# High and low parts of a 128-column operand side by side in one matmul of 256 columns, in the attention heads of a two-block fp32 kernel

## The chip, the cores and the metric

One core of one Trainium2 chip runs the whole program. The metric is the device time of one execution in microseconds (us); lower is better. The chip's engines have an instruction stream each, run in program order, and wait for one another by semaphores: TensorE (PE in the rows: matmuls, PEld its weight loads), VectorE (DVE), ScalarE (ACT), GpSimd (POOL) and SyncE (SP), which here issues the transfers from memory.

## The reference

Two blocks on 256 tokens of width 1024, all in fp32. The first has differential attention (4 heads) beside block attention (8 heads, called moba), gates, and a gated per-layer input. The second has two layers of retention (4 heads, two blocks of 128 queries) beside stick-breaking attention (8 heads), and an MLP. Cut to what the change touches:

```python
def diff_attention(q, k, v, lam, ...):        # per head and query block
    a = softmax(where(causal, q @ k * scale, -inf))      # two maps, m = 0, 1
    w = a[:, :, 0] - lam * a[:, :, 1]
    o = rms_norm(w @ v, subln_g) * (1 - lam_init)

def retention(q, k, v, log_gamma):             # per head and 128-token chunk
    inner = ((q @ k) * decay) @ v
    cross = (q @ state) * q_decay

def stick_breaking(q, k, v):                   # per head
    z = q @ k * scale
    log_1m_beta = where(causal, log_sigmoid(z) - z, 0)
    after = reverse_cumsum(log_1m_beta) - log_1m_beta
    out = where(causal, exp(log_sigmoid(z) + after), 0) @ v
```

## The kernel before

**Numbers.** Every operand of a matmul is a sum of a high part (the value rounded to fp32r) and a low part (the rest). `hilo` makes them: ScalarE copies (line 131), VectorE subtracts (line 132). A product is then three matmuls, high x high, high x low, low x high, summed in PSUM; `mm3` (lines 139 to 142) issues them.

**Weights.** They come as 189 chunks of 1 MB into three buffers (`raw`), fetched by SyncE. Two chunks ahead of its use a chunk is split into `wh` (ScalarE, line 302) and `wl` (VectorE, line 303), with three buffers each. The chunk's matmuls (line 137) go into accumulators of one PSUM bank each (`acc`, five banks); a 512-column matmul multiplies a weight by high and low parts of the activations, which lie side by side, and one of 256 by the high part alone. The two halves of the bank are added afterwards: a ScalarE copy (line 337) and a VectorE addition (line 338), which make `f`.

**Heads.** The other three PSUM banks (`aux`) belong to the attention heads. Each head is a Python generator that is stepped once per chunk; its steps lie between `yield`s. `soft_head` (4 differential and 8 moba heads, one per 128 lanes), `ret_head` (8) and `sb_head` (16, 8 in each layer).

- A stick-breaking head: scores z by two `mm3`, 256 and 128 columns (two key blocks, causal); a mask added on both diagonal blocks; |z|, exp, ln on ScalarE; high and low part (`ph`, `pl`); then matmuls with a triangle and a vector of -1 (lines 796, 797: the reverse sum) into the same bank; an exponential; high and low part; values by two `mm3` (256 and 128 columns); and their high and low part into `B`, k = h for head h. `B` is what the chunk matmuls of p_sb multiply, all eight k's, so that heads 6 and 7 are waited for at k = 6 and 7.
- A differential head: values by `mm3` for each of three 128 x 128 blocks; squares with a sum (line 544, ScalarE reading PSUM), a power on GpSimd, scaling (line 548), and transposes (line 553).

**Order.** The program is handed to a scheduler that decides the order on each engine from a timeline that it computes itself. A change of a few instructions so moves many others. ScalarE's functions need tables; sigmoids need another one than exp and ln, and `act` emits the table load (line 116) ahead of the first one. The order of the functions with tables is kept as written.

Of the kernel before, what the change touches and what calls it, by code (L numbers as in the profile page):

```python
# [22 lines left out]
PB = 2  # L23
# [57 lines left out]
def tile_blocks(ctx: ExitStack, tc: tile.TileContext, a: dict, out: bass.AP):  # L81
# [61 lines left out]


# [13 lines left out]
    msk = tl([384], "msk")  # L158
    tri_f = tl([P], "sig", bufs=4)
# [9 lines left out]
    m_sb = msk[:, None, 2 * P:3 * P].to_broadcast([P, 2, P])  # L169
# [7 lines left out]
    def late_consts():  # L177
        load(cst, a["tables"][:, 0:C_SB])
        load(msk, a["tables"][:, C_SB:C_TRI])
        load(tri_f, a["tables"][:, C_TRI:C_DEC])  # L180
        load(lamv, a["lambdas"].rearrange("(o i e) -> o i e", o=1, e=64).to_broadcast([P, 4, 64]))

    def use_consts():
        V.tensor_mul(gfm, g_fin, g_mix[0])
        V.tensor_scalar_mul(subg, subg, 1.0 - LAM_INIT)
        V.tensor_copy(tri, tri_f)
        V.tensor_scalar_mul(neg1, ones, -1.0)
# [40 lines left out]
    def sums(sq, cols=True):  # L228
        h, l = tl([S], "ph", F32R, 2), tl([S], "pl", F32R, 2)
# [215 lines left out]
    def head_rows():  # L445

        for _ in range(3):
            yield
        ps = aux()[:, 0:S]
        for h in range(2):  # L450
            dh, dl = tl([P], "ph", F32R, PB), tl([P], "pl", F32R, PB)
# [40 lines left out]
    def soft_head(idx, j, v, diff, wait):  # L492
# [33 lines left out]
        wh, wl = tl([2, 384], "ph", F32R, 2), tl([2, 384], "pl", F32R, 2)  # L526
# [8 lines left out]
        if diff:  # L535
            po = aux()[:, 0:S].rearrange("p (h e) -> p h e", h=2)
            h, l = wh[:, 0], wl[:, 0]
            vc = slice(j * P, (j + 1) * P)
            for i, (o, qt, kt) in enumerate(BLK):
                mm3(po[:, qt], h[:, o:o + P], l[:, o:o + P], vh[:, kt, vc], vl[:, kt, vc], i == 0, qt == kt)  # L540
            o = o_slot[idx % 2]
            ss = tl([2], "ss", bufs=2)
            for h in range(2):
                A.activation(o[:, h], po[:, h], AF.Square, accum_out=ss[:, h:h + 1])
            V.tensor_scalar(ss, ss, 1.0 / 128, EPS5, ALU.mult, ALU.add)
            G.tensor_tensor(ss, ss, mhalf[:, 0:2], ALU.pow)
            for h in range(2):
                A.activation(o[:, h], po[:, h], AF.Copy, scale=ss[:, h:h + 1])
# [193 lines left out]
    def ret_head(h, j, qk, v, L):  # L742
        (qh, ql), (kh, kl) = qk
# [3 lines left out]
        mm3(ps[:, 256:384], kh[:, j, 128:256], kl[:, j, 128:256], qh[:, j, 128:256], ql[:, j, 128:256], False, True)  # L747
        t = tl([384], "t", bufs=2)
        V.tensor_mul(t, ps[:, 0:384], L.dec[:, 384 * h:384 * (h + 1)])
        dh, dl = tl([384], "ph", F32R, 2), tl([384], "pl", F32R, 2)  # L750
# [26 lines left out]
    def sb_head(h, j, qk, v, L):  # L777
        (qh, ql), (kh, kl) = qk
# [3 lines left out]
        mm3(z[:, 256:384], kh[:, j, 128:256], kl[:, j, 128:256], qh[:, j, 128:256], ql[:, j, 128:256], False, True)  # L782
        zd = z.rearrange("p (b s) -> p b s", b=2)[:, :, 0:P]
        V.tensor_add(zd, zd, m_sb)
# [6 lines left out]
        h2, l2 = tl([2, 384], "ph", F32R, 2), tl([2, 384], "pl", F32R, 2)  # L791
        h_, l_ = h2[:, 0], l2[:, 0]
# [7 lines left out]
        h_, l_ = h2[:, 1], l2[:, 1]  # L800
        hilo(h_, l_, t)
        yield
        po = aux()[:, 0:S]
        e = slice(h % 4 * P, (h % 4 + 1) * P)
        mm3(po, vh[:, 0, e], vl[:, 0, e], h_[:, 0:256], l_[:, 0:256], True, True)
        mm3(po[:, 128:256], vh[:, 1, e], vl[:, 1, e], h_[:, 256:384], l_[:, 256:384], False, True)
# [3 lines left out]
    def layer(l):  # L810
# [32 lines left out]
        for u in range(2):  # L843
# [3 lines left out]
            def ev(ps, h, u=u):  # L847
# [294 lines left out]
```

## Time and profile before

| | |
|---|---|
| time, median of three runs | 1152.4 us (1151.77 to 1152.56) |
| the profiled execution | 1152.48 us, its span 1150.5 us, mean granted clock 0.998 |
| TensorE busy | 1139.5 us (99%), 6579 matmuls |
| VectorE, ScalarE, GpSimd busy | 874.3 (76%), 717.7 (62%), 221.6 us (19%) |
| moved by DMA | 207.70 MB, mean 181 GB/s |

The span is the time between the first and the last instruction that the profile holds; some 2 us lie around it. The matmul's own time in the rows contains its way through the array, some 0.2 to 0.3 us, in which the next one already runs. What a matmul costs in a stream is the distance from its start to the next start.

### The profile page before, as it was taken

Reading aid. Unit: us, or ns where it says so; the run is one execution under the profiler, and the core shown is the slowest. Engines: PE = TensorE matmul, PEld = TensorE weight load, DVE = VectorE, ACT = ScalarE, POOL = GpSimd, SP = SyncE. Lnnn points to the kernel's source line nnn. Section 1 sums busy time; section 2 is a strip of 40 time slices with the busy share of each in tenths; the row PEclk is TensorE's granted clock in tenths of the full one; section 3 lists DMA queues with packets and bytes.
Section 4 is the critical chain, followed back from the end, with each engine's and each line's share of the span. In section 5 each row is a group of like instructions: output and inputs, shape, how many; then the busy total and the mean of one; then the engine's idle time right before and its main releaser. Section 6 shows DMA issues by size and latency. Waiting matters only on the chain.

```text
span 1150.5 us, 17428 instructions
## 1 busy us (share of the span) xinstructions
PE 1139.5 (99%) x6579; PEld 998.6 (87%) x6579; DVE 874.3 (76%) x1457; ACT 717.7 (62%) x1302; POOL 221.6 (19%) x236
## 2 busy tenths in 40 slices
PE   8999999999999999999999999999999999999997
PEld 6888899998888888888888888888898888888887
DVE  6867777689978867778876777978776767967664
ACT  7777955476567776556654645556776555856452
POOL 0021241036532122110000013641121312000001
PEclk9999999999999999999999999999999999999999
DMA  8644345556544445545555556455444654555551
GB/s 320 235 152 144 138 170 197 183 179 220 183 179 151 174 152 183 184 158 209 184 190 189 193 197 216 171 189 183 147 147 146 214 189 165 212 188 185 188 178 37
DMA packets 33028, 207.70 MB, mean 181 GB/s; under 512 B 3888, under 2 KB 6576, under 8 KB 8880
## 3 DMA queue, kind: packets, MB, share of 16 engines
q1 hardware_dynamic: 32944, 206.59, 50.9%
q8 instruction: 52, 0.85, 0.3%
q14 instruction: 32, 0.26, 0.1%
HBM read 203.42 MB, written 1.05 MB: 178 GB/s over the span
## 4 chain that ended last, share of the span: by engine, by line
PE 91%; DVE 4%; DMA 2%; ACT 2%; issue 1%; POOL 0%; SPq 0%; POOLq 0%; DVEq 0%
PE acc L137 80%; DVE wl L303 2%; PE acc L142 1%; PE acc L141 1%; PE acc L140 1%; PE aux L142 1%; PE aux L141 1%; PE aux L140 1%; DMA M<-in_xn_dram 1%; DVE X L688 1%; PE aux L797 1%; PE aux L501 1%; ACT wh L302 0%; POOL sig L838 0%; DMA X<-in_xt_dram 0%
## 5 line engine op out<-in xcount | busy, mean ns | idle before, releaser
L303 DVE TENSOR_TENSOR wl<-raw,wh 128x1024 fp32r<-128x1024 f32 (+1 forms) x382 | 466.3, 1248 | 114.4 <-ACT wh L302 111.8
L302 ACT ACTIVATE wh<-raw 128x1024 fp32r<-128x1024 f32 (+1 forms) x382 | 381.2, 1043 | 190.8 <-PE acc L137 159.2
L137 PE MATMUL acc<-X,wh 128*128 128x512 f32 x1472 | 382.9, 394 | 0.6 <-DVE X L688 0.4
L137 PEld LDWEIGHTS acc<-X,wh 128*128 128x128 f32 x1472 | 263.8, 189 | 49.0 <-issue 1.2
L137 PE MATMUL acc<-X,wl 128*128 128x256 f32 x1472 | 220.7, 283 | 0.0
L137 PEld LDWEIGHTS acc<-X,wl 128*128 128x128 f32 x1472 | 207.2, 190 | 14.1
L337 ACT ACTIVATE f<-acc 128x256 f32<-128x256 f32 x216 | 79.3, 374 | 69.1 <-PE acc L137 68.8
L137 PE MATMUL acc<-wh,X 128*128 128x512 f32 x448 | 118.8, 394 | 0.6 <-ACT wh L302 0.5
L338 DVE TENSOR_TENSOR f<-f,acc 128x256 f32<-128x256 f32 x216 | 87.3, 414 | 30.2 <-ACT f L337 29.3
L137 PEld LDWEIGHTS acc<-wh,X 128*128 128x128 f32 x448 | 83.3, 189 | 18.4 <-ACT wh L302 1.9
L220 POOL TENSOR_TENSOR sq<-sq,f 128x256 f32<-128x256 f32 x24 | 27.6, 1150 | 263.9 <-ACT f L218 263.7
L688 DVE TENSOR_TENSOR X<-X,acc 128x256 f32<-128x256 f32 x112 | 45.8, 416 | 34.2 <-PE acc L137 33.5
L619 POOL TENSOR_TENSOR sig<-f,nr 128x256 f32<-128x256 f32 x48 | 44.7, 940 | 120.1 <-DVE f L338 85.8
L137 PE MATMUL acc<-B,wh 128*128 128x512 f32 x256 | 64.7, 392 | 0.0
L137 PE MATMUL acc<-A,wh 128*128 128x512 f32 x256 | 64.4, 392 | 0.0
L137 PE MATMUL acc<-wl,X 128*128 128x512 f32 x224 | 64.4, 395 | 0.0
L137 PEld LDWEIGHTS acc<-B,wh 128*128 128x128 f32 x256 | 46.1, 189 | 8.2
L137 PE MATMUL acc<-M,wh 128*128 128x512 f32 x192 | 52.9, 393 | 0.0
L137 PEld LDWEIGHTS acc<-A,wh 128*128 128x128 f32 x256 | 45.9, 189 | 8.1
L137 PEld LDWEIGHTS acc<-wl,X 128*128 128x128 f32 x224 | 41.7, 188 | 9.1 <-DVE wl L303 1.0
L137 PEld LDWEIGHTS acc<-M,wh 128*128 128x128 f32 x192 | 35.0, 188 | 6.8
L568 POOL TENSOR_TENSOR G<-f,nr 128x256 f32<-128x256 f32 x24 | 22.7, 946 | 84.3 <-DVE f L338 83.9
(236 smaller groups left out, 1652.9 us busy)
## 6 DMA issues: line engine op xcount, KB each, us to landing
raw<-in_wstream_dram SPq DMA_DIRECT2D x187, 1024.0 KB, 4.8
sig<-f SPq DMA_DIRECT2D x32, 64.0 KB, 5.1
B<-in_tables_dram SPq DMA_DIRECT2D x2, 768.0 KB, 5.1
raw<-in_wstream_dram SPq DMA_DIRECT2D x4, 256.0 KB, 4.8
raw<-in_wstream_dram SPq DMA_DIRECT2D x2, 512.0 KB, 7.6
M<-in_xn_dram SPq DMA_DIRECT2D x1, 1024.0 KB, 11.4
out_dram<-M SPq DMA_DIRECT2D x4, 256.0 KB, 2.2
X<-in_xt_dram SPq DMA_DIRECT2D x3, 256.0 KB, 6.6
```

Source lines behind the costliest of these rows:

```text
L137: last[0] = T.matmul(*args, **kw)
L140: T.matmul(o, lhsT=lh, rhs=rh, start=start, stop=False, skip_group_check=True)
L141: T.matmul(o, lhsT=lh, rhs=rl, start=False, stop=False, skip_group_check=True)
L142: T.matmul(o, lhsT=ll, rhs=rh, start=False, stop=stop, skip_group_check=True)
L220: (V if k == KT - 1 else G).tensor_add(sq, sq, t)
L302: h = A.activation(ch.wh[:, k], ch.raw[:, k], AF.Copy)
L303: l = V.tensor_sub(ch.wl[:, k], ch.raw[:, k], f32(ch.wh[:, k]))
L337: A.activation(t, ps[:, S:2 * S], AF.Copy)
L338: V.tensor_add(t, t, ps[:, 0:S])
L568: G.tensor_mul(dst()[:, k], fold(ps), st.n.rb)
L619: G.tensor_mul(store[(c, i)][0][:, k % 2], fold(ps), st.n.rb)
L688: V.tensor_add(X[:, k], X[:, k], ps[:, o:o + S])
```

## The change

`mm2` takes the place of `mm3` where the moving operand has 128 columns. High and low part of that operand lie side by side ("ph" holds both now, the values too), and one matmul of 256 columns multiplies them by the stationary high part; its result is 256 columns wide, with the high product in one half and the low one in the other. A second matmul of 128 columns adds the product of the stationary low part. The two halves are summed behind it: `add_up` (ScalarE copies 128 columns, VectorE adds) in retention scores and stick-breaking values; in the stick-breaking scores a ScalarE copy into the tile "msb", a GpSimd addition of the mask to it, and the VectorE addition that was there before reads this tile; in the differential values a copy of 256 columns and an addition, after which the squares and the scaling read SBUF and not PSUM. The mask is loaded in a transfer of its own, 64 KB.

Score blocks of 8 retention and 16 stick-breaking heads, values of 16 stick-breaking heads, and values of 4 differential heads (three blocks each) are so changed. The moba heads are not.

```diff
+    def parts():
+
+        return tl([2, 2, 384], "ph", F32R, 2)
...
+    def mm2(o, o0, lh, ll, r, rh, start, stop):
+
+        T.matmul(o, lhsT=lh, rhs=r, start=start, stop=False, skip_group_check=True)
+        T.matmul(o0, lhsT=ll, rhs=rh, start=False, stop=stop, skip_group_check=True)
+
+    def add_up(o, ex, t):
+
+        A.activation(t, ex, AF.Copy)
+        V.tensor_add(o, o, t)
...
-    m_sb = msk[:, None, 2 * P:3 * P].to_broadcast([P, 2, P])
+    m_sb = tl([2, P], "msb")
...
-            po = aux()[:, 0:S].rearrange("p (h e) -> p h e", h=2)
+            po = aux().rearrange("p (h c e) -> p h c e", h=2, c=2)
...
-                mm3(po[:, qt], h[:, o:o + P], l[:, o:o + P], vh[:, kt, vc], vl[:, kt, vc], i == 0, qt == kt)
+                mm2(po[:, qt], po[:, qt, 0], h[:, o:o + P], l[:, o:o + P], v.v.t[:, kt, :, vc], vh[:, kt, vc],
+                    i == 0, qt == kt)
             o = o_slot[idx % 2]
             ss = tl([2], "ss", bufs=2)
+            A.activation(o, po[:, :, 1], AF.Copy)
+            V.tensor_add(o, o, po[:, :, 0])
+            q2 = tl([S], "ft", bufs=2)
             for h in range(2):
-                A.activation(o[:, h], po[:, h], AF.Square, accum_out=ss[:, h:h + 1])
+                A.activation(q2[:, h * P:(h + 1) * P], o[:, h], AF.Square, accum_out=ss[:, h:h + 1])
...
-                A.activation(o[:, h], po[:, h], AF.Copy, scale=ss[:, h:h + 1])
+                A.activation(o[:, h], o[:, h], AF.Copy, scale=ss[:, h:h + 1])
...
     def ret_head(h, j, qk, v, L):
...
-        mm3(ps[:, 256:384], kh[:, j, 128:256], kl[:, j, 128:256], qh[:, j, 128:256], ql[:, j, 128:256], False, True)
+        mm2(ps[:, 256:512].rearrange("p (c q) -> p c q", c=2), ps[:, 384:512], kh[:, j, 128:256], kl[:, j, 128:256],
+            qt_[:, j, :, 128:256], qh[:, j, 128:256], False, True)
         t = tl([384], "t", bufs=2)
+        add_up(ps[:, 256:384], ps[:, 384:512], t[:, 0:P])
...
     def sb_head(h, j, qk, v, L):
...
-        mm3(z[:, 256:384], kh[:, j, 128:256], kl[:, j, 128:256], qh[:, j, 128:256], ql[:, j, 128:256], False, True)
-        zd = z.rearrange("p (b s) -> p b s", b=2)[:, :, 0:P]
-        V.tensor_add(zd, zd, m_sb)
+        mm2(z[:, 256:512].rearrange("p (c q) -> p c q", c=2), z[:, 384:512], kh[:, j, 128:256], kl[:, j, 128:256],
+            qt_[:, j, :, 128:256], qh[:, j, 128:256], False, True)
+        zd, ms = z.rearrange("p (b s) -> p b s", b=2)[:, :, 0:P], m_sb
+        A.activation(ms[:, 1], z[:, 384:512], AF.Copy)
+        G.tensor_add(ms[:, 1], ms[:, 1], ms[:, 0])
+        V.tensor_add(zd, zd, ms)
...
-        mm3(po[:, 128:256], vh[:, 1, e], vl[:, 1, e], h_[:, 256:384], l_[:, 256:384], False, True)
+        mm2(p3[:, 128:384].rearrange("p (c q) -> p c q", c=2), p3[:, 256:384], vh[:, 1, e], vl[:, 1, e],
+            hl[:, 1, :, 256:384], h_[:, 256:384], False, True)
+        add_up(po[:, 128:256], p3[:, 256:384], tl([384], "t", bufs=2)[:, 0:P])
```

**Where instructions move.** Three places of the order on the engines follow. In the changed program line 140 is the chunk matmul, 143 to 145 are `mm3`, 149 and 150 `mm2`, 825 and 826 the triangular products, 134 and 135 `hilo`.

First, TensorE at the end of the stick-breaking heads of the first layer, before the change: aux_701 is the bank of head 7's values, acc_721 and acc_723 are the accumulators that multiply B, and acc_728, acc_731 and acc_736 belong to chunks that multiply X.

```order
L140 MATMUL aux_701_4530<-ph_680_4399,vh_638_4116 128x128
L141 MATMUL aux_701_4530<-pl_681_4400,vh_638_4116 128x128
L142 MATMUL aux_701_4530<-ph_680_4399,vl_639_4117 128x128
L137 MATMUL acc_728_4708<-X2_369_2428,wl_711_4591 128x256 x3
L137 MATMUL acc_731_4730<-X2_369_2428,wh_710_4590 128x512 x8
L137 MATMUL acc_731_4730<-X2_369_2428,wl_711_4591 128x256 x8
L137 MATMUL acc_721_4651<-B2_573_3683,wh_702_4539 128x512
L137 MATMUL acc_723_4676<-B2_573_3683,wh_702_4539 128x512
L137 MATMUL acc_736_4759<-X2_369_2428,wh_718_4643 128x512 x4
L137 MATMUL acc_721_4651<-B2_573_3683,wh_702_4539 128x512
L137 MATMUL acc_721_4651<-B2_573_3683,wl_703_4540 128x256 x8
L137 MATMUL acc_723_4676<-B2_573_3683,wh_702_4539 128x512
```

The same place in the changed program, from the last triangular product of head 7 on: aux_682 and aux_684 hold the values of heads 6 and 7, acc_705 and acc_707 multiply B, and the first row for B is k = 6, as is the second.

```order
L826 MATMUL aux_661_4384<-ph_663_4398,tri_10_73 128x384
L140 MATMUL acc_720_4761<-X2_363_2420,wl_703_4646 128x256 x5
L143 MATMUL aux_682_4519<-ph_660_4381,vh_623_4111 128x256
L144 MATMUL aux_682_4519<-ph_660_4381,vh_623_4111 128x256
L145 MATMUL aux_682_4519<-ph_660_4381,vh_623_4111 128x256
L149 MATMUL aux_682_4519<-ph_660_4381,vh_623_4111 128x256
L150 MATMUL aux_682_4519<-ph_660_4381,vh_623_4111 128x128
L143 MATMUL aux_684_4530<-ph_663_4398,vh_623_4111 128x256
L144 MATMUL aux_684_4530<-ph_663_4398,vh_623_4111 128x256
L145 MATMUL aux_684_4530<-ph_663_4398,vh_623_4111 128x256
L149 MATMUL aux_684_4530<-ph_663_4398,vh_623_4111 128x256
L150 MATMUL aux_684_4530<-ph_663_4398,vh_623_4111 128x128
```

The rows that come next are the two k = 6 matmuls of B and then the k = 7 one. The chunk matmuls on X that stood between the values and B (and between the triangular products and the values) now stand ahead of the triangular products.

Second, ScalarE at the same place in the changed program, from the exponential of head 6 (t_672) and of head 7 (t_673) on. The four sig tiles are gates; ph_663 is head 7's high part.

```order
L117 ACTIVATE t_672_4456<-aux_658_4367 128x384
L134 ACTIVATE ph_660_4381<-t_672_4456 128x384
L117 ACTIVATE t_673_4464<-aux_661_4384 128x384
L115 ACT_TABLE_LOAD
L117 ACTIVATE sig_650_4317<-sig_650_4317 128x512
L117 ACTIVATE sig_668_4426<-sig_668_4426 128x512
L117 ACTIVATE sig_678_4493<-sig_678_4493 128x512
L117 ACTIVATE sig_690_4566<-sig_690_4566 128x512
L134 ACTIVATE ph_663_4398<-t_673_4464 128x384
L154 ACTIVATE t_683_4525<-aux_682_4519 128x128
L134 ACTIVATE B2_559_3671<-aux_682_4519 128x256
L154 ACTIVATE t_685_4536<-aux_684_4530 128x128
```

Here is what stood there before, with head 6's and head 7's high parts ph_676 and ph_680.

```order
L118 ACTIVATE t_690_4458<-aux_674_4369 128x384
L118 ACTIVATE t_691_4466<-aux_678_4386 128x384
L116 ACT_TABLE_LOAD
L118 ACTIVATE sig_668_4323<-sig_668_4323 128x512
L131 ACTIVATE ph_676_4382<-t_690_4458 128x384
L118 ACTIVATE sig_686_4428<-sig_686_4428 128x512
L118 ACTIVATE sig_696_4495<-sig_696_4495 128x512
L337 ACTIVATE f_715_4618<-acc_713_4598 128x256
L118 ACTIVATE sig_706_4564<-sig_706_4564 128x512
L131 ACTIVATE ph_680_4399<-t_691_4466 128x384
```

Head 6's high part moved ahead of the table load; head 7's stands behind all four sigmoids in both orders, and the copies of line 154 are new.

Third, TensorE behind the values of the last differential head (aux_173 before), up to its transposes into aux_188.

```order
L142 MATMUL aux_173_977<-vh_79_440,pl_158_899 128x128
L137 MATMUL acc_179_1003<-wl_149_841,X2_13_76 128x512 x4
L137 MATMUL acc_179_1003<-wh_148_840,X2_13_76 128x512 x4
L137 MATMUL acc_178_1002<-wh_162_920,X2_13_76 128x512 x4
L137 MATMUL acc_178_1002<-wl_163_921,X2_13_76 128x512 x4
L137 MATMUL acc_178_1002<-wh_162_920,X2_13_76 128x512 x3
L553 MATMUL aux_180_1028<-cst_2_62,B2_15_78 128x128 x2
L137 MATMUL acc_178_1002<-wh_162_920,X2_13_76 128x512
L484 MATMUL aux_181_1034<-cst_2_62,sig_165_940 128x128 x4
L137 MATMUL acc_179_1003<-wh_162_920,X2_13_76 128x512 x4
L137 MATMUL acc_179_1003<-wl_163_921,X2_13_76 128x512 x4
L137 MATMUL acc_179_1003<-wh_162_920,X2_13_76 128x512 x4
```

Four more transposes of line 484 come next, and then those into aux_188. In the changed program the values are in aux_171 and the transposes go into aux_186 (line 576; line 502 is what line 484 was).

```order
L149 MATMUL aux_171_974<-vh_79_442,ph_156_896 128x256
L150 MATMUL aux_171_974<-vh_79_442,ph_156_896 128x128
L576 MATMUL aux_179_1025<-cst_2_62,B2_17_80 128x128 x2
L502 MATMUL aux_180_1031<-cst_2_62,sig_163_937 128x128 x4
L140 MATMUL acc_178_1000<-wl_161_918,X2_15_78 128x512 x2
L140 MATMUL acc_178_1000<-wh_160_917,X2_15_78 128x512 x4
L502 MATMUL aux_181_1038<-cst_2_62,sig_164_938 128x128 x4
L576 MATMUL aux_186_1082<-cst_2_62,B2_17_80 128x128
```

Between the values and these transposes 27 matmuls of 512 columns stood before, and 6 stand now. ScalarE's part of this chain in the changed program, from the new copy (line 563) over the squares (line 567) to the scaling (line 571), is this.

```order
L563 ACTIVATE B2_17_80<-aux_171_974 128x256
L431 ACTIVATE vh_185_1065<-acc_177_999,hr_30_148 128x512
L134 ACTIVATE M2_33_161<-aux_180_1031 128x2x256
L567 ACTIVATE ft_173_984,ss_172_981<-B2_17_80 128x128 x2
L134 ACTIVATE A2_19_82<-ft_152_878 128x256
L431 ACTIVATE vh_185_1065<-acc_178_1000,hr_30_148 128x512
L318 ACTIVATE wh_192_1118<-raw_162_923 128x1024 x2
L134 ACTIVATE M2_33_161<-aux_181_1038 128x2x256
L571 ACTIVATE B2_17_80<-B2_17_80,ss_172_981 128x128 x2
```

The copy is new, and two more evacuations of accumulators (line 431, 134) have come between the squares' input and the scaling than stood there before.

## Rows read from the trace of the kernel before

**Rows 1.** The page's first part: busy time, share of the span, instructions
```profile
PE 1139.5 (99%) x6579; PEld 998.6 (87%) x6579; DVE 874.3 (76%) x1457; ACT 717.7 (62%) x1302; POOL 221.6 (19%) x236
```
**Rows 2.** The chain that ended last, share of the span by engine
```profile
PE 91%; DVE 4%; DMA 2%; ACT 2%; issue 1%; POOL 0%; SPq 0%; POOLq 0%; DVEq 0%
```
**Rows 3.** Waits of TensorE, longest first: total us, times, longest
```profile
PE aux L428 <- DVE one_r L167: 1.3, 1, 1.3
...
PE aux L140 <- ACT M L131: 0.2, 1, 0.2
```
**Rows 4.** Timeline of TensorE, second layer's scores: start us, us, instruction
```profile
858.90 0.22 PE L140 MATMUL aux<-M 128*128 128x128 f32 x1
...
859.07 0.27 PE L142 MATMUL aux<-M 128*128 128x128 f32 x1
859.18 0.34 PE L141 MATMUL aux<-pl,vh 128*128 128x256 f32 x1
859.35 0.28 PE L142 MATMUL aux<-ph,vl 128*128 128x256 f32 x1
```
**Rows 5.** Timeline of TensorE, a moba head's values
```profile
135.22 0.28 PE L141 MATMUL aux<-pl,vh 128*128 128x256 f32 x1
135.34 0.28 PE L142 MATMUL aux<-ph,vl 128*128 128x256 f32 x1
```
**Rows 6.** Groups by line and shape, ScalarE: busy us, mean ns
```profile
L337 ACT ACTIVATE f<-acc 128x256 f32<-128x256 f32 x216 | 79.3, 374 | 69.1 <-PE acc L137 68.8
...
L544 ACT ACTIVATE B<-aux 128x128 f32<-128x128 f32 x8 | 2.1, 273 | 1.8 <-PE aux L142 1.8
```
**Rows 7.** Timeline of TensorE, first layer, end of the stick-breaking heads
```profile
425.63 0.39 PE L797 MATMUL aux<-pl,tri 128*128 128x384 f32 x1
...
440.08 0.39 PE L137 MATMUL acc<-B,wh 128*128 128x512 f32 x1
```
**Rows 8.** Timeline of ScalarE, the same stretch
```profile
425.66 0.89 ACT L118 ACTIVATE t<-aux 128x384 f32<-128x384 f32 x2 [1.85 <-PE aux L797]
426.57 1.28 ACT L116 ACT_TABLE_LOAD   x1
...
428.81 1.14 ACT L118 ACTIVATE sig<-sig 128x512 f32<-128x512 f32 x2
...
430.64 0.51 ACT L131 ACTIVATE ph<-t 128x384 fp32r<-128x384 f32 x1
...
435.69 0.38 ACT L131 ACTIVATE B<-aux 128x256 fp32r<-128x256 f32 x1 [0.90 <-PE aux L142]
```
**Rows 9.** Timeline of VectorE, the same stretch
```profile
431.19 0.79 DVE L132 TENSOR_TENSOR pl<-t,ph 128x384 fp32r<-128x384 f32 x1 [0.45 <-ACT ph L131]
...
436.11 0.43 DVE L132 TENSOR_TENSOR B<-aux,B 128x256 fp32r<-128x256 f32 x1 [0.86 <-ACT B L131]
```
**Rows 10.** Timeline of TensorE, second layer, end of the stick-breaking heads
```profile
870.14 0.39 PE L797 MATMUL aux<-pl,tri 128*128 128x384 f32 x1
...
888.09 0.40 PE L137 MATMUL acc<-B,wh 128*128 128x512 f32 x1
```
**Rows 11.** Timeline of TensorE, the last differential head
```profile
92.07 0.27 PE L142 MATMUL aux<-vh,pl 128*128 128x128 f32 x1
...
100.67 0.38 PE L553 MATMUL aux<-cst,B 128*128 128x128 f32 x2
```
**Rows 12.** Timeline of ScalarE, the last differential head
```profile
94.27 2.01 ACT L302 ACTIVATE wh<-raw 128x1024 fp32r<-128x1024 f32 x2 [0.96 <-PE acc L137]
96.19 0.60 ACT L548 ACTIVATE B<-aux,ss 128x128 f32<-128x128 f32 x2
97.23 0.69 ACT L414 ACTIVATE vh<-acc,hr 128x512 fp32r<-128x512 f32 x1 [0.43 <-PE acc L137]
97.81 0.59 ACT L131 ACTIVATE M<-aux 128x512 fp32r<-128x512 f32 x1
```
**Rows 13.** Engines by stretch: us, busy of each, granted clock, DMA share
```profile
23.60:25.20 1.60, 0.51 (x4) 0.11 (x3) 1.23 (x7) 1.60 (x4) 0.00 (x0) 1.00 1.00 415
```

More of the change, by code (lines that the diff above doesn't have):

```diff
@@ L22 @@
 GW = 64
-PB = 2
 S = 256
@@ L157, in tile_blocks @@
     cst = tl([C_SB], "cst")
-    msk = tl([384], "msk")
-    tri_f = tl([P], "sig", bufs=4)
+    msk = tl([2 * P], "msk")
+    tri_f, ms_f = tl([P], "sig", bufs=4), tl([P], "sig", bufs=4)
     ident = cst[:, C_ID:C_ID + P]
@@ L178, in late_consts @@
         load(cst, a["tables"][:, 0:C_SB])
-        load(msk, a["tables"][:, C_SB:C_TRI])
+        load(msk, a["tables"][:, C_SB:C_MS])
+        load(ms_f, a["tables"][:, C_MS:C_TRI])
         load(tri_f, a["tables"][:, C_TRI:C_DEC])
@@ L186, in use_consts @@
         V.tensor_copy(tri, tri_f)
+        G.tensor_copy(m_sb[:, 0], ms_f)
         V.tensor_scalar_mul(neg1, ones, -1.0)
@@ L228, in sums @@
     def sums(sq, cols=True):
-        h, l = tl([S], "ph", F32R, 2), tl([S], "pl", F32R, 2)
+        hl = parts()
+        h, l = hl[:, 0, 0, 0:S], hl[:, 0, 1, 0:S]
         hilo(h, l, sq)
@@ L409, in __init__ @@
         def __init__(self):
-            self.h, self.l = tl([2, 512], "vh", F32R), tl([2, 512], "vl", F32R)
+            self.t = tl([2, 2, 512], "vh", F32R)
+            self.h, self.l = self.t[:, :, 0], self.t[:, :, 1]
         def evac(self, ps, h):
@@ L450, in head_rows @@
         for h in range(2):
-            dh, dl = tl([P], "ph", F32R, PB), tl([P], "pl", F32R, PB)
+            hl = parts()
+            dh, dl = hl[:, 0, 0, 0:P], hl[:, 0, 1, 0:P]
             A.activation(dh, ident, AF.Copy, scale=n0.rc[h])
@@ L525, in soft_head @@
         yield
-        wh, wl = tl([2, 384], "ph", F32R, 2), tl([2, 384], "pl", F32R, 2)
+        hl = parts()
+        wh, wl = hl[:, :, 0], hl[:, :, 1]
         for m in range(1 if diff else 2):
@@ L742, in ret_head @@
     def ret_head(h, j, qk, v, L):
-        (qh, ql), (kh, kl) = qk
+        (qh, ql), (kh, kl), qt_ = qk
         vh, vl = v.h, v.l
@@ L746, in ret_head @@
         mm3(ps[:, 0:256], kh[:, j, 0:128], kl[:, j, 0:128], qh[:, j], ql[:, j], True, True)
-        mm3(ps[:, 256:384], kh[:, j, 128:256], kl[:, j, 128:256], qh[:, j, 128:256], ql[:, j, 128:256], False, True)
+        mm2(ps[:, 256:512].rearrange("p (c q) -> p c q", c=2), ps[:, 384:512], kh[:, j, 128:256], kl[:, j, 128:256],
+            qt_[:, j, :, 128:256], qh[:, j, 128:256], False, True)
         t = tl([384], "t", bufs=2)
+        add_up(ps[:, 256:384], ps[:, 384:512], t[:, 0:P])
         V.tensor_mul(t, ps[:, 0:384], L.dec[:, 384 * h:384 * (h + 1)])
-        dh, dl = tl([384], "ph", F32R, 2), tl([384], "pl", F32R, 2)
+        hl = parts()
+        dh, dl = hl[:, 0, 0], hl[:, 0, 1]
         hilo(dh, dl, t)
@@ L777, in sb_head @@
     def sb_head(h, j, qk, v, L):
-        (qh, ql), (kh, kl) = qk
+        (qh, ql), (kh, kl), qt_ = qk
         vh, vl = v.h, v.l
@@ L790, in sb_head @@
         V.scalar_tensor_tensor(t, zz, 0.0, t, ALU.max, ALU.add)
-        h2, l2 = tl([2, 384], "ph", F32R, 2), tl([2, 384], "pl", F32R, 2)
-        h_, l_ = h2[:, 0], l2[:, 0]
+        hl = parts()
+        h_, l_ = hl[:, 0, 0], hl[:, 0, 1]
         hilo(h_, l_, t)
@@ L799, in sb_head @@
         act(t, zz, AF.Exp)
-        h_, l_ = h2[:, 1], l2[:, 1]
+        h_, l_ = hl[:, 1, 0], hl[:, 1, 1]
         hilo(h_, l_, t)
         yield
-        po = aux()[:, 0:S]
+        p3 = aux()
+        po = p3[:, 0:S]
         e = slice(h % 4 * P, (h % 4 + 1) * P)
         mm3(po, vh[:, 0, e], vl[:, 0, e], h_[:, 0:256], l_[:, 0:256], True, True)
-        mm3(po[:, 128:256], vh[:, 1, e], vl[:, 1, e], h_[:, 256:384], l_[:, 256:384], False, True)
+        mm2(p3[:, 128:384].rearrange("p (c q) -> p c q", c=2), p3[:, 256:384], vh[:, 1, e], vl[:, 1, e],
+            hl[:, 1, :, 256:384], h_[:, 256:384], False, True)
+        add_up(po[:, 128:256], p3[:, 256:384], tl([384], "t", bufs=2)[:, 0:P])
         hilo(L.b.h[:, h], L.b.l[:, h], po)
@@ L824, in sl, with qkt @@
             return L.m.h[:, i:i + 2], L.m.l[:, i:i + 2]
+        def qkt(u):
+            i = 4 * (u % 2)
+            return sl(u, 0), sl(u, 1), L.m.t[:, i:i + 2]
         def rot_evac(w_):
@@ L852, in ev @@
                     for j in range(2):
-                        threads.append(ret_head(2 * u + j, j, (sl(u, 0), sl(u, 1)), L.v[u], L))
+                        threads.append(ret_head(2 * u + j, j, qkt(u), L.v[u], L))
             chunk_n(w, 2 + u, x_, ev)
@@ L873, in sb_start @@
             for j in range(2):
-                threads.append(sb_head(2 * u + j, j, (sl(u, 0), sl(u, 1)), L.v[2 + u // 2], L))
+                threads.append(sb_head(2 * u + j, j, qkt(u), L.v[2 + u // 2], L))
         for u in range(4):
```

## Prediction

> **What bounds the kernel now.** I read the page from the top. TensorE is busy for 1139.5 of 1150.5 us [rows 1], and the chain that ended last runs through it for 91% of the span [rows 2]: the engine is to be seen as the bound, not as one of several. The view of what TensorE waited for has seven rows that add up to 4.5 us, none above 1.3 us and none in a head's second half [rows 3]. So whatever takes columns or starts off TensorE comes off the time almost one for one, and whatever makes TensorE wait is added one for one, because nothing behind it has slack to give back. The other engines (VectorE 76%, ScalarE 62%, GpSimd 19% busy) matter only where TensorE would have to wait for them. After that I read the starts of neighbouring matmuls, which tell what a shape costs in a stream, and then the stretches in which TensorE comes closest to its producers: the ends of the stick-breaking heads and of the last differential head.
>
> **What the change takes off TensorE.** Three matmuls of 128 columns become one of 256 and one of 128. The groups are 24 second score blocks (8 retention, 16 stick-breaking heads), 16 stick-breaking value blocks and 12 differential value blocks (4 heads, 3 blocks each): 52.
>
> In [rows 4] three 128-column matmuls stand in a row. From the first start to the start of the next shape 859.18 - 858.90 = 0.28 us pass, and that next one, 256 columns, keeps the engine 0.17 us (859.35 - 859.18) where it keeps it 0.12 us behind another of 256 [rows 5]. So a group costs 0.28 + 0.05 = 0.33 us. The last two of the three start 0.11 us apart (859.07 to 859.18), about as far as two of 256 columns: halving the columns did not halve the price. The new pair is one start of 256 at 0.12 and one of 128 at 0.11, 0.23 us. It saves 0.10 us, 52 times: **-5.2 us**. The bounds: if the single 128 streamed at half the 256's price (0.06) the pair would be 0.18 and the saving 7.8 us; if it paid the 0.05 of the next one once more, 0.28 and 2.6 us.
>
> The Trainium skill, page "TensorE: Matmul & The Clock Gate", section "Back-to-back issue gap", gives the isolated spacing of two matmuls as the columns divided by the clock plus 2.5 ns. By that alone the change would save nothing but 52 of these 2.5 ns, since 3 x 128 columns equal 256 + 128. The same section says that in a stream the weight load counts too, and [rows 4] agree with that part: 0.11 us for 128 columns is what a start costs there, not half of 0.12.
>
> **What it adds on other engines.** In all, 40 ScalarE copies of 128 columns (8 retention, 16 masks, 16 stick-breaking values) at 0.27 us, from the nearest row, a read of 128 x 128 out of PSUM, and 4 of 256 columns at 0.37 [rows 6], together 12.3 us; 28 more VectorE additions, some 9 us at the same prices; 16 GpSimd additions of masks, of a size that no row here has. None of these engines is full, so the sum of it costs nothing; the place does. Early in a stick-breaking head the chain grows by the copy and the GpSimd addition, 0.27 and, between ScalarE's price and four times as much, 0.3 to 1.1: 0.6 to 1.4 us, and the listing of the new order puts about 4 to 5 us more of chunk work between a head's scores and its triangular products than before. In a retention head the two steps (0.6 us) also have chunk matmuls in front of them. These I cost at nothing; without the cover they would cost up to 1.4 us a head. One constant (the triangle) now waits behind one more weight chunk at the start; it is first used in the second block, and I put 0.2 us (0 to 0.4) for what VectorE, which casts it in program order, hands on.
>
> **Where a wait comes in: the end of stick-breaking, first layer.** In the kernel before, the last triangular product starts at 425.63 and the last use of B for head 7 comes at 440.08 [rows 7]. Between them ScalarE does the exponential, a table load of 1.28, four sigmoids at 0.54 or so (two in 1.14), the high part of head 7 at 430.64 to 431.15 [rows 8], VectorE the low part to 431.98 [rows 9], and after the values ScalarE the high part of B to 436.07. B is there by about 436.5, so 3.5 us of slack.
>
> In the new order, quoted above, the chunk matmuls that filled this stretch stand ahead of the triangular products. From the last triangular start T, TensorE has 0.23 (this product) + 5 x 0.12 + 2 x 0.59 (values of heads 6 and 7, each four starts of 0.12 and one of 0.11) + 2 x 0.23 (B of head 6) = 2.5 us until it needs B of head 7. ScalarE has, by [rows 8]: the exponential ends at T + 0.9; table load, T + 2.2; four sigmoids, which all stand ahead of the high part now, T + 4.4; high part, T + 4.9. The low part takes VectorE to T + 5.6. The values of head 7 then end at about T + 6.35 as ScalarE sees it, the added copy takes 0.27, the added sum 0.3, the high part of B 0.38, the low part 0.42: T + 7.9. TensorE waits 7.9 - 2.5 = **5.4 us**, some 4 of them at the values of head 7. Nothing passes it, since the engine works in order. Late next: ScalarE's evacuation of these accumulators, with a weight split of 2.0 us between the two of them, so that the next chunk but one waits for its bank, 0.5 (0 to 1.2).
>
> **The same, second layer.** Before, the last triangular product started at 870.14 and the last B at 888.09 [rows 10]. In the new order the table load and four sigmoids again precede head 7's high part; TensorE has 4.9 us of work from the last triangular start T to B of head 7 here (some 2.4 us more than in the first layer), so the chain alone, 7.9 us, would leave a wait of 3.0. But a weight split (2.0 us) stands between the two heads' exponentials on ScalarE. If its buffer is free when ScalarE comes to it, it ends some 1.1 us behind the product of head 7, and the wait is 4.1; if it needs the chunk matmuls just behind that product to end first, it ends 2.2 us behind, and the wait is 5.2. I take **4.6**, and 0.5 (0 to 1.2) for the bank as above.
>
> **The last differential head.** Before, its values end at 92.2, and its transposes come at 100.67 [rows 11]; the scaled output was ready at 96.9 [rows 12]. In the new order the transposes stand 2.5 us behind the values (six short transposes, six matmuls of 0.23, four transposes). ScalarE has, in its new order: copy 0.37, a value evacuation 0.69, a high part 0.60, two squares 0.27 each, a high part 0.4, an evacuation 0.69, a split in two halves 2.0, a high part 0.60, one scaling 0.36; overlapping as in [rows 12] that is 5.5 to 5.9. The wait is 3.0 to 3.4, or 1.4 if the split was done early; I take **3.0**.
>
> **Sum.** -5.2 + 0.2 + 5.4 + 0.5 + 4.6 + 0.5 + 3.0 = +9.0 us. The profiled execution is 1152.48 (1150.5 and 2.0 around it), the median of three runs 1152.4: 1152.5 + 9.0 = **1161.5**. With the small ends (first layer 4.5, if the four hops between engines there cost nothing; second 4.1; differential 1.4; no bank waits; saving 5.2) it is 1157.3; with the large ones (5.4 + 1.2, 5.2 + 1.2, 3.4, 0.4 at the start, saving 2.6) it is 1166.7. That is this case's own range. A difference under 0.2%, 2.3 us, can't be told from none here.
>
> **Rivals.**
> *The saving stays.* If ScalarE reaches head 7 earlier than its row-by-row sum says, TensorE keeps the 5.2 us: 1147.4. For it: the kernel before has the same chain, and shows no wait. Against it: its cover was chunk work between the triangular products and B (up to 440.08 in [rows 7]), which the new listing has ahead. It decides at 2.9 us: if the three places together cost less, the kernel is faster by more than can be missed. 17%.
>
> *Half is given back.* One sb end waits as worked out, or both do so for half: waits of 3 to 7.5 us, 1150.5 to 1154.8, no difference. For it: the hops between engines are known here to 0.1 or 0.2 us each only, and there are eight in a chain. 13%.
>
> *Nothing saved on TensorE.* If columns alone set the pace, the waits stand without the 5.2: 1166.7. [Rows 4] speak against it, 0.11 for 128 columns beside 0.12 for 256. 4%.
>
> *The clock falls in the waits.* The longest idle stretch that shows, 1.1 of 1.6 us at 23.6, kept a granted clock of 1.00, the 2.4 GHz level [rows 13]; waits of 4 us in one piece are not in this trace. If each of three were followed by 2 us of matmuls at 1.2 GHz, each would cost 1 more: 1164.5; at 4 us, 1167.5. The same page of the Trainium skill, section "Part 1: The HAM clock gate", states that an idle TensorE goes back to the lower level; no run here shows it so far. 10%.
>
> The main case has the rest, 56%. Slower by over 0.2%: 56 + 4 + 10 = 70%; within: 13%; faster: 17%. A range of 1149 to 1167 leaves out most of the first rival and part of the last two, 2 in 10.
>
> **What will show it.** The view of TensorE's waits should have new rows: values of the sb heads on the low part (about 4 us, twice), B on its low part, and transposes of the differential output on the scaling (about 3). The four sigmoids should stand between the exponential and the high part of head 7 without a break on ScalarE. A 256-column matmul of second blocks should be followed after 0.12, and the 128 after 0.11. TensorE's busy time should fall by about 5. I am wrong if these waits are missing or each under 1 us, or if busy time doesn't fall.

## The result, and the profile after

The changed kernel takes 1166.84 us (median of four runs, 1165.85 to 1168.36), the kernel before 1152.38 (four runs): a ratio of 1.0127, 95% interval 1.0115 to 1.0139, so 14.5 us slower where 9.0 were forecast. The profiled execution took 1165.85 us, its span is 1163.8, 13.3 more than before.

The page's first part, busy time by engine, of the changed kernel, beside [rows 1]:

```profile
PE 1140.8 (98%) x6527; PEld 996.0 (86%) x6527; DVE 882.5 (76%) x1485; ACT 728.1 (63%) x1346; POOL 229.2 (20%) x253
```

TensorE issues 52 matmuls less and yet is busy 1.3 us longer. That is the first thing to be explained. The second is idle time: these are its waits in the changed kernel (total us, times, longest), six of eleven rows, beside [rows 3].

```profile
PE aux L143 <- ACT ph L134: 5.2, 2, 3.4
PE aux L576 <- ACT B L571: 3.2, 1, 3.2
PE aux L519 <- DVE ft L585: 1.6, 1, 1.6
PE acc L140 <- DVE f L354: 1.6, 3, 0.9
...
PE acc L140 <- DVE B L135: 1.0, 3, 0.4
...
PE aux L144 <- DVE ph L135: 0.4, 2, 0.2
```

All rows add up to 16.5 us, 12.0 more than before. The rows to see are the first two: the values of head 7 wait on their high part in both layers (3.4 and 1.9 us), the last differential transposes on the scaling (3.2).

TensorE's timeline at the first layer's tail in the changed kernel, the place of [rows 7]:

```profile
441.54 0.39 PE L826 MATMUL aux<-ph,tri 128*128 128x384 f32 x1
441.77 0.75 PE L140 MATMUL acc<-X,wl 128*128 128x256 f32 x5
...
442.83 0.22 PE L150 MATMUL aux<-ph,vh 128*128 128x128 f32 x1
446.42 0.38 PE L143 MATMUL aux<-ph,vh 128*128 128x256 f32 x1 [3.38 <-ACT ph L134]
447.02 0.38 PE L144 MATMUL aux<-ph,vh 128*128 128x256 f32 x1 [0.21 <-DVE ph L135]
...
448.10 1.08 PE L140 MATMUL acc<-B,wh 128*128 128x512 f32 x2 [0.40 <-DVE B L135]
449.33 0.79 PE L140 MATMUL acc<-B,wh 128*128 128x512 f32 x1 [0.15 <-DVE B L135]
```

And ScalarE there, the place of [rows 8]:

```profile
441.97 0.49 ACT L117 ACTIVATE t<-aux 128x384 f32<-128x384 f32 x1 [0.74 <-PE aux L826]
442.48 1.28 ACT L115 ACT_TABLE_LOAD   x1
443.77 2.19 ACT L117 ACTIVATE sig<-sig 128x512 f32<-128x512 f32 x4
445.87 0.51 ACT L134 ACTIVATE ph<-t 128x384 fp32r<-128x384 f32 x1
...
447.79 0.28 ACT L154 ACTIVATE t<-aux 128x128 f32<-128x128 f32 x1 [0.20 <-PE aux L150]
448.44 0.38 ACT L134 ACTIVATE B<-aux 128x256 fp32r<-128x256 f32 x1 [0.37 <-DVE aux L155]
```

With T = 441.54, the last triangular product's start, the high part ends at T + 4.84 and B of head 7 is used at T + 7.8. The forecast, from the rows of before in the new order, had T + 4.9 and T + 7.9. VectorE's low part came at 446.40 for 0.56 us.

At the second layer's tail the values of head 7 wait like this:

```profile
900.63 0.39 PE L143 MATMUL aux<-ph,vh 128*128 128x256 f32 x1 [1.87 <-ACT ph L134]
```

There the last triangular product starts at 894.69, a weight split on ScalarE runs from 894.30 to 896.30, and B of head 7 is used at 903.54, which is T + 8.85.

The last differential head in TensorE's timeline (before: [rows 11]):

```profile
98.42 0.60 PE L502 MATMUL aux<-cst,sig 128*128 128x128 f32 x4
102.18 0.33 PE L576 MATMUL aux<-cst,B 128*128 128x128 f32 x1 [3.17 <-ACT B L571]
```

and in ScalarE's (before: [rows 12]), where the added copy, the split and the scaling stand in one unbroken row:

```profile
96.55 0.38 ACT L563 ACTIVATE B<-aux 128x256 f32<-128x256 f32 x1 [2.42 <-PE aux L150]
...
99.34 2.01 ACT L318 ACTIVATE wh<-raw 128x1024 fp32r<-128x1024 f32 x2
...
101.71 0.71 ACT L571 ACTIVATE B<-B,ss 128x128 f32<-128x128 f32 x2
```

Now the busy time. Stretches of the changed kernel (us; busy of PE, PEld, DVE, ACT, POOL; the granted clock is the third number from the end), to be read beside [rows 13]:

```profile
99.00:102.00 3.00, 0.01 (x1) 0.00 (x0) 2.75 (x6) 3.00 (x5) 0.79 (x1) 1.00 0.23 98
102.00:104.00 2.00, 1.82 (x15) 1.46 (x16) 1.97 (x7) 0.65 (x3) 0.00 (x0) 0.88 0.21 33
104.00:106.00 2.00, 2.00 (x7) 1.41 (x6) 0.80 (x7) 1.98 (x9) 0.00 (x0) 0.50 0.82 319
106.00:108.00 2.00, 2.00 (x13) 1.80 (x12) 0.48 (x1) 1.99 (x5) 0.00 (x0) 0.76 0.41 172
...
448.00:450.00 2.00, 1.75 (x4) 0.94 (x5) 0.77 (x3) 0.46 (x2) 0.00 (x0) 0.57 0.00 0
450.00:452.00 2.00, 2.00 (x11) 1.95 (x10) 0.00 (x0) 0.13 (x1) 0.00 (x0) 0.58 0.00 0
...
900.00:910.00 10.00, 8.66 (x41) 6.92 (x41) 5.39 (x11) 5.82 (x15) 0.15 (x1) 0.83 0.20 84
```

Some 1.4 to 1.9 us after TensorE has resumed, the granted clock falls to 0.50, the 1.2 GHz level, and comes back. TensorE is busy meanwhile but for short waits behind the first tail, with half the matmuls in the same time (7 from 104 to 106, where the kernel e2 below has 14 at 1.00). What is lost, at most, is the time times the missing share: 2 x (0.12 + 0.50 + 0.24) = 1.7 us behind the differential head, 2 x (0.43 + 0.42) = 1.7 behind the first tail, 10 x 0.17 = 1.7 behind the second. Together 5.1. No other stretch of 10 us in this kernel has a lower clock, apart from the end; before, only the end had.

The last reading is the price of the pair. TensorE's timeline of the last differential values in the changed kernel:

```profile
95.70 0.28 PE L149 MATMUL aux<-vh,ph 128*128 128x256 f32 x1
95.82 0.22 PE L150 MATMUL aux<-vh,ph 128*128 128x128 f32 x1
95.88 0.33 PE L149 MATMUL aux<-vh,ph 128*128 128x256 f32 x1
96.05 0.22 PE L150 MATMUL aux<-vh,ph 128*128 128x128 f32 x1
96.11 0.34 PE L149 MATMUL aux<-vh,ph 128*128 128x256 f32 x1
```

From pair to pair it is 0.23 us (95.88 to 96.11). The 128 is followed after 0.06 and lengthens the next start from 0.12 to 0.17, which is the same 0.11 as forecast, shown in two places. So 52 pairs save 5.2 us by their starts. The sum is 12.0 more idle, 5.1 for the clock, less 5.2, and 1.4 that neither row holds; 13.3 in all. A wait costs more than its idle time: behind 0.40 us of idle at 448.10 the last start was 0.62 us back where it would be 0.06 in a stream. A matmul's own time in the rows is 0.16 us longer than its step in a stream (0.28 beside 0.12; the 0.2 to 0.3 given ahead of the prediction is too much), and the idle time starts only behind it. Worked out like this at every wait, waits cost some 3.5 us beyond their idle time in the changed kernel and some 1.8 before; the difference, 1.7, covers the 1.4. This is an estimate.

### The profile page after: what moved, and what is told of

Its sections match the earlier page's. It is cut to its first block, busy times and chain, and to the rows that moved or that the text cites. A ratio compares the mean times of both kernels' runs of the same rounds, so it can differ in the third digit from the quotient of the medians.

```text
span 1163.8 us, 17466 instructions
## 1 busy us (share of the span) xinstructions
PE 1140.8 (98%) x6527; PEld 996.0 (86%) x6527; DVE 882.5 (76%) x1485; ACT 728.1 (63%) x1346; POOL 229.2 (20%) x253
## 4 chain that ended last, share of the span: by engine, by line
PE 87%; DVE 6%; ACT 4%; DMA 1%; issue 1%; POOL 1%; SPq 0%; POOLq 0%; DVEq 0%; ACTq 0%
PE acc L140 77%; DVE wl L319 3%; PE acc L144 1%; PE acc L145 1%; PE acc L143 1%; ACT wh L318 1%; DMA M<-in_xn_dram 1%; DVE X L711 1%; PE aux L145 1%; PE aux L143 1%; PE aux L144 1%; PE aux L826 1%; PE aux L149 1%; PE aux L519 0%; ACT L115 0%
## 5 line engine op out<-in xcount | busy, mean ns | idle before, releaser
L135 DVE TENSOR_TENSOR ph<-t,ph 128x384 fp32r<-128x384 f32 x40 | 28.5, 723 | 17.2 <-ACT ph L134 16.9
```

What stands on the lines that cost most here:

```text
L135: V.tensor_sub(lo, src, f32(hi))
```

## Experiments

The theory (W below): the pairs save what they should, three waits in TensorE's order and a stretch at the lower clock behind each take more. The rivals: the loss is added work spread over the blocks; or the clock costs nothing of its own. Each kernel was timed in five rounds beside the kernel before (1152.1 to 1152.3 us).

**e1.** ScalarE's order is fixed for heads 6 and 7, nothing else:

```diff
+        if keep:
+            tc.stamp_issue_order_token(ins.ins, "act_table")
...
-        hilo(h_, l_, t)
+        hilo(h_, l_, t, h > 5)
...
-        add_up(po[:, 128:256], p3[:, 256:384], tl([384], "t", bufs=2)[:, 0:P])
-        hilo(L.b.h[:, h], L.b.l[:, h], po)
+        add_up(po[:, 128:256], p3[:, 256:384], tl([384], "t", bufs=2)[:, 0:P], h > 5)
+        hilo(L.b.h[:, h], L.b.l[:, h], po, h > 5)
```

> As changed, but on ScalarE the high part, the add-up copy and the B copy of stick-breaking heads 6 and 7 are kept in one written order with the functions with tables, so that the table load and the four sigmoids stand behind B. Theory W (the extra time is TensorE's waits at three places and a stretch at the lower clock behind each): the waits at the values (3.4 and 1.9 us) fall to 0.6 or less, B and then a bank are waited for about 2 us in each layer in their place, and no stretch at 1.2 GHz is left behind them; some 6 to 9 us less than as changed: 1158 to 1161. Theory C (the waits are covered somewhere else, the loss is added work on all heads): within 2 us of 1166.8.

Measured: 1160.93 us, ratio 1.0077 (1.0064 to 1.0091), 5.9 less than as changed. TensorE's waits in e1, the first three of nine rows:

```profile
PE acc L142 <- DVE f L358: 3.5, 5, 1.1
PE aux L580 <- ACT B L575: 3.2, 1, 3.2
PE acc L142 <- DVE B L137: 2.2, 4, 1.0
```

The waits at the values are gone, the differential one (line 580 here) is untouched, and shorter ones on B and on the accumulators' evacuation, which now stands behind the sigmoids, came in their place. Apart from the end, the only lower clock left is behind the differential head (0.83 over 100 to 110). All waits together are 14.9 us, only 1.6 less than as changed; the two stretches of lower clock that are gone (up to 3.4) are most of the 4.8 us by which the profile is shorter. This fits W: a new order of a dozen ScalarE instructions, with all the added work still there, takes 40% of the loss away.

**e2.** Matmuls that nobody reads, put into the waits:

```diff
+        if h == 7:
+            for _ in range(30 if L.l == 0 else 16):
+                T.matmul(p3[:, 384:512], lhsT=tri, rhs=neg1, start=True, stop=True, skip_group_check=True)
...
+            if idx == 3:
+                for _ in range(28):
+                    T.matmul(pa[:, S:S + P], lhsT=tri, rhs=neg1, start=True, stop=True, skip_group_check=True)
```

> As changed, with matmuls of 128 columns whose result nobody reads, placed into TensorE's waits: 28 ahead of the last differential head's transposes, 30 and 16 ahead of the values of head 7 in the two layers. Theory W with the clock as a cost of its own: ScalarE's and VectorE's chains end when they did, but the granted clock stays at 1.00 behind the waits; about 1.7 us less at each of three places, 1161 to 1163. If the clock costs nothing of its own: 1166.8 or more by what of the filling lies beyond the waits (0 to 2 us).

Measured: 1161.59 us, ratio 1.0087 (1.0074 to 1.0101): 5.3 us less with 74 matmuls more. The same stretches in e2:

```profile
99.00:102.00 3.00, 3.00 (x30) 3.00 (x28) 2.75 (x6) 3.00 (x6) 0.80 (x1) 1.00 0.29 120
...
104.00:106.00 2.00, 2.00 (x14) 1.78 (x14) 0.93 (x8) 1.98 (x9) 0.00 (x0) 1.00 0.78 287
...
448.00:450.00 2.00, 2.00 (x16) 1.87 (x15) 1.01 (x3) 1.53 (x3) 0.00 (x0) 1.00 0.00 0
```

VectorE and ScalarE are as busy from 99 to 102 as without the filling, so their chain takes as long; what changed is the clock behind it. The order around the filling moved a little too (the wait at line 519 is 0.8 us shorter), so of the 5.3 some 0.8 is not the clock's; by the place, at equal numbers of chunk matmuls, TensorE gains 2.5, 1.4 and 1.0 us in the profile. Without the 0.8 the clock is worth 1.7, 1.4 and 1.0 us: less than 1.7 at the two tails, where at the full clock TensorE waits 0.50 us for B of head 7 instead (0.15 and nothing as changed). The rival on the clock falls.

**e3.** The differential part undone, the rest as changed:

```diff
-                mm2(po[:, qt], po[:, qt, 0], h[:, o:o + P], l[:, o:o + P], v.v.t[:, kt, :, vc], vh[:, kt, vc],
-                    i == 0, qt == kt)
+                mm3(po[:, qt], h[:, o:o + P], l[:, o:o + P], vh[:, kt, vc], vl[:, kt, vc], i == 0, qt == kt)
...
-            A.activation(o, po[:, :, 1], AF.Copy)
-            V.tensor_add(o, o, po[:, :, 0])
```

> As changed, with the differential values as before (three matmuls, squares and scaling from PSUM); 40 groups are left changed. Theory W: the wait ahead of the last transposes (3.2 us), what follows it and the clock behind it are gone, 1.2 us of saving too: about 4 us less, 1162 to 1163.5. Theory C: a third of the loss at most goes, 1165 or more.

Measured: 1162.53 us, ratio 1.0091 (1.0077 to 1.0105), 4.3 less than as changed. The order of this place is again that of before, with 32 chunk matmuls ahead of the transposes (the rows of before ahead of the prediction add up to 32 too, where the text there says 27), and the wait of 3.2 us does not appear; the 5.3 us of line 143 do:

```profile
PE aux L143 <- ACT ph L134: 5.3, 2, 3.4
```

The clock behind the differential head stays at 1.00. But behind the first tail, behind the same wait of 3.38 us, the lower clock lasts twice as long as in the whole change and takes 10 x 0.34 = 3.4 us:

```profile
440.00:450.00 10.00, 6.92 (x26) 5.66 (x27) 3.05 (x8) 5.22 (x12) 1.41 (x2) 0.66 0.13 53
```

**e4.** e1 and e3 together, no other edit.

> Both at once: the order of e1 and the differential values as before. Theory W: the two add up, 1154 to 1157, between the two kernels, with about 4 us saved by the 40 pairs and some 4 to 6 of waits left. Theory C: above 1163.

Measured: 1156.90 us, ratio 1.0041 (1.0028 to 1.0053); 9.9 less than as changed, where e1 and e3 alone gave 5.9 and 4.3. They add up, so these are separate places. 4.8 us of loss stay, at a clock of 1.00 but for the end: the waits add up to 10.1 us, 5.6 more than before, most of them the shorter ones that e1 also has.

**e5.** The kernel before with the pairs in the stick-breaking scores alone (the `mm3` lines of retention scores and of both kinds of values are back; as in e6 and e7, made from the changed kernel, the tile that holds high and low part and the mask's own transfer stay):

> The kernel before, with the new matmuls in the 16 stick-breaking score blocks alone. In its order the chunk matmuls of the two tails stand ahead of the triangular products, as in the whole change (2.1 and 5.1 us of work from the end of the last one to B of head 7; before 14.4 and 16.8). Theory W (what costs is the order that the longer score chain brings about): nearly the whole loss of the stick-breaking part, 1160 to 1164. Rival (each changed block costs its share): 16 of the 40 blocks of e3 bring 16/40 of its 10.4 us, 1156.

Measured: 1164.51 us, ratio 1.0103 (1.0088 to 1.0118), 12.2 us lost with 16 pairs, half a us more than expected and more than the 10.4 of e3 with 40. Its waits begin with

```profile
PE aux L143 <- ACT ph L134: 4.7, 2, 3.2
```

and its clock is 0.83 over 440 to 450 and 0.69 over 900 to 910. The rival that each block costs its share falls: what costs is the order, and the edit of the scores is what turns it over. Which part of that edit does it, no run separates: the copy, the GpSimd addition, and the one tile "msb" that all 16 heads share came together.

**e6.** The kernel before with the pairs in retention scores and stick-breaking values alone:

> The kernel before, with the new matmuls in the 8 retention score blocks and the 16 stick-breaking value blocks alone, their added copies and additions included. In its order 9.8 us or more of work stand between the last triangular product and B of head 7, more than the chain's 7.9. Theory W: no new wait, no lower clock, and 24 x 0.10 saved: 1149.5 to 1150.5. Rival (the added copies and additions cost, or the pairs save nothing): 1152 or more.

Measured: 1152.40 us, ratio 1.0002 (0.9993 to 1.0011). A miss: there is no long wait and no lower clock, as expected, but the 2.4 us are not there either. Of its waits, these two are those at the tails that before does not have, or not of this size (another, 0.9 on a weight split, lies at 6.4 us, at the program's start):

```profile
PE acc L140 <- DVE B L135: 1.1, 1, 1.1
...
PE acc L140 <- DVE f L354: 0.7, 2, 0.5
```

Set beside the kernel before at equal numbers of chunk matmuls, TensorE is ahead by 1.4 us at 420 us, which the pairs explain (4 of retention and some 8 of values), and 1.3 behind at 455: the first tail took 2.7. At the end of the program it is only 0.1 behind: the 12 pairs of the second layer did save their 1.2 us, 0.10 each, and no new wait came there. In the first layer the 9.8 us of work that I had counted in front of B stood at the wrong place. The values of head 7 come late in TensorE's order, right in front of B:

```profile
440.47 0.22 PE L150 MATMUL aux<-ph,vh 128*128 128x128 f32 x1
440.53 0.68 PE L140 MATMUL acc<-B,wh 128*128 128x512 f32 x2
442.33 0.50 PE L140 MATMUL acc<-B,wh 128*128 128x512 f32 x1 [1.12 <-DVE B L135]
```

Only the two matmuls of head 6's B stand between, and the copy, the sum, the high and the low part that follow the values take until 442.27. Before, the last value started at 435.38 and B of head 7 at 440.08, with chunk matmuls between.

**e7.** The kernel before with the pairs in the differential values alone:

> The kernel before, with the new matmuls in the 12 differential value blocks alone. Theory W: the 3.2 us wait ahead of the last transposes, what follows it, and the stretch at 1.2 GHz, less 1.2 us of saving: 1155 to 1157. Rival (the loss there needs the other parts): 1151 to 1152.

Measured: 1158.30 us, ratio 1.0051 (1.0038 to 1.0063), 6.0 us for 12 pairs, 1.3 us more than expected: the same 3.2 us wait, and two falls of the clock, one behind it and one behind a wait of 1.7 at the block heads' scores (rows at the end).

**e8.** The changed kernel with the stick-breaking scores as before and a third `yield` between a differential head's scaling and its transposes. Two heads share an output slot, and a later head writes it before these transposes read it, so the time is that of the same instructions on other data.

> The changed kernel with the stick-breaking scores as before, and with the transposes of a differential head one chunk later (a third yield between scaling and transposes), so that chunk matmuls stand in front of them in its order. 36 pairs. Theory W: no wait above 1.5 us, clock 1.00 throughout, 36 x 0.10 = 3.7 us saved, 1148 to 1149.5. Rival (a pair saves less inside the whole, or a new wait comes behind the later transposes): 1150 to 1153.

Measured: 1159.42 us, ratio 1.0060 (1.0047 to 1.0073). A miss, but one that the shared slot makes: the second of the four heads' transposes wait for the scaling of the last head, which writes the slot that they read (99.91 to 100.59 on ScalarE, line 571). They start at 100.35, behind 2.0 us of idle. The last head's own transposes come at 112.20 without a wait, as theory W has it. The clock is 0.66 over 100 to 110, and 0.83 over 130 to 140 behind a wait of 1.7 us at the block heads' scores: up to 5.1 us. What this order would take with a slot for each head was not run.

**e9 and e10.** e6 with the order of e1 on ScalarE; and this with the pairs in the scores of heads 0 and 1 of each layer as well (`if h < 2` around the `mm2`, `mm3` otherwise).

> The 24 pairs of e6 (retention scores, stick-breaking values), with the written order of e1 on ScalarE, so that B of head 7 no longer stands behind the table load and the four sigmoids. Theory W (e6 gained nothing because a 1.1 us wait on B and the bank and split waits behind it took back its 2.4 us): the wait on B falls below 0.4, and 1.0 to 2.0 us stay, 1150.4 to 1151.4. Rival (24 pairs save less than 1 us, or the folds behind the sigmoids wait in B's place): 1152 to 1153.5.

> As e9, and the pair in the stick-breaking scores of heads 0 and 1 of each layer too (28 pairs); in its order 9.5 to 10.4 us of work stand between the last triangular product and B of head 7. Theory W: 1150.0 to 1151.0, 0.4 less than e9. Rival: 1152 to 1154.

Measured: 1152.89 us, ratio 1.0005 (0.9996 to 1.0014), and 1155.12, ratio 1.0025 (1.0015 to 1.0035). The rival of e9 holds; e10 lies above both of its ranges. Waits of e9:

```profile
PE acc L142 <- DVE f L358: 1.8, 3, 1.2
...
PE acc L142 <- DVE B L137: 0.3, 1, 0.3
```

The wait on B is down to 0.3; the accumulators' folds (the additions that make `f`) stand behind table load and sigmoids, and TensorE waits for these instead, 1.6 us in the first layer. Again the second layer keeps its 1.2 us. The clock stays at 1.00 but for the end. No kernel here is faster than the one before.

## Why the prediction came out as it did

- **The saving** (5.2 from 0.10 a pair) was right: 0.23 from pair to pair, and 1.2 us for 12 pairs in the second layer of e6. The isolated spacing that the Trainium skill gives ("TensorE: Matmul & The Clock Gate", section "Back-to-back issue gap") would have left next to nothing here. The trace, with 0.11 us for 128 columns, disagrees with that spacing for this stream; the section itself says that it under-counts there at few columns.
- **First tail**, 5.4 and 0.5 forecast: 3.4 + 0.2 at the values, 0.6 on B, 0.9 for the bank, 5.1 idle. From start to start, B of head 7 came 7.8 - 2.5 = 5.3 late. Right in place, in cause (e1) and in size; the parts of ScalarE's sum met their rows within 0.1 us.
- **Second tail**, 4.6 and 0.5 forecast: 1.9 + 0.2 + 0.4 + 0.5 = 3.0 idle. From start to start it is 8.85 - 4.9 = 3.9 and the bank: some of it is not idle time but the distance that a wait adds, and matmuls at the lower clock. The weight split ended 1.2 us behind the product of head 7; that is the early one of the two cases, forecast at 4.1. So the middle of the two was over-sized by 0.7.
- **Differential head**, 3.0 forecast: 3.2, and 0.8 more at the block heads' scores behind it, which I had not looked at. e3 gives 4.3 for the whole part.
- **The clock.** This is the step that failed. "The clock falls in the waits" stood among the rivals at 10%, with 1 us a place in its cheaper version and 2 in the other, and the main case had nothing for it. It came at all three places, up to 1.7 us each and 5.1 together; e2, which keeps TensorE at work there, is 5.3 us faster, 4.1 of its profile's gain by the clock. With it the forecast sum, 9.0 + 5.1, is 14.1 for 13.3 in the profile and 14.5 in the medians; that it meets them so closely is partly luck, since the second tail was too large and the wait at the block heads' scores was missing. I had given it 10% because an idle row of before (1.1 of 1.6 us) kept 1.00; a row of a third of the length was no evidence for waits of 3 us and more. The Trainium skill, "TensorE: Matmul & The Clock Gate", section "Part 1: The HAM clock gate", says that the engine goes back to the lower level when idle: the trace agrees in that 0.50 is granted behind waits of 3.4, 3.2 and 1.9 us, but it comes there only after TensorE has resumed.
- **The sign.** The prediction called itself wrong "if busy time doesn't fall". It rose by 1.3 us, where -5 was forecast: the pairs did take their 5.2 off, and the lower clock put about as much back on.
- **The early part of the heads**, forecast at nothing, did cost nothing where it stands: no wait on a score of these heads or on a triangular product is among the new rows. But e5 shows what it does elsewhere: with the edit of the scores the scheduler puts the fillers ahead. I had read this effect in the listing without asking which edit causes it.
- The forecast that half could be given back, or the saving kept, fell with the result. e6 and e9 show that even without the scores' pairs the first layer's tail takes the saving back.

What stays open: which part of the scores' edit turns the order, what e8 takes with a slot for each head, and why the same wait is followed by 1.7 us of lost clock in one kernel, by 3.4 or by none in another.

## What to carry to other kernels

On a kernel that TensorE bounds, a cheaper matmul form is priced by the distance between starts, and then by the steps that its result needs before anyone can read it: find the last consumer in the new order, add up the row of instructions on the engine that feeds it, and compare with the work that is left in front. Where this leaves TensorE idle for some us in one piece, count the lower clock behind it as well (in the whole change up to 1.7 us a place, beside 3.0 to 5.1 us of idle time; in e3, e5 and e8 up to 3.4 at one place). A written order on the feeding engine, or filling matmuls, gave back some 40% of the loss each, but the short waits of the written order moved on to the next buffer.

## What the runs showed of the hardware that was not expected

- The lower clock comes behind the wait, not in it. It is granted at 1.00 through the idle time and for a while after TensorE has resumed, 1.4 to 1.9 us in the whole change and 0.2 to 3.4 over all kernels here; then it is 0.50 while the engine works, and it returns. Apart from the end of each program, nine such stretches took up to 1.7 us each, and three (the first tail of e3, the second of e5, the differential head of e8) up to 3.4.
- The length of the wait alone does not settle it. A wait of 1.65 us at 128.49 in the whole change was followed by a clock of 1.00 throughout; in e7 the same wait, 1.66 us at 128.26, was followed by this stretch:

```profile
128.00:130.00 2.00, 1.74 (x15) 1.48 (x16) 1.94 (x7) 1.99 (x8) 0.15 (x1) 0.89 0.01 4
130.00:132.00 2.00, 2.00 (x7) 1.51 (x6) 1.84 (x10) 2.00 (x8) 0.54 (x1) 0.50 0.69 238
132.00:134.00 2.00, 2.00 (x12) 1.86 (x11) 1.27 (x4) 2.00 (x10) 0.89 (x2) 0.75 0.68 287
```

So a kernel with such a wait can take 1.7 us more or not.

- Executions of one kernel differ in this too. The four of the whole change had mean granted clocks of 0.995 (1165.85 and 1166.83 us), 0.993 (1166.84) and 0.992 (1168.36); the profiled one is the fastest, so its three stretches are not those of every execution.
